# A block of experts computed by 64 rows each with unsplit weights, and a 17th block

## The chip, the core and the metric

The kernel runs on one core of one Trainium2 chip. The metric is the device time of one execution in microseconds (us). TensorE is called PE here, VectorE DVE, ScalarE ACT, GpSimd POOL and SyncE SP; PEld is PE's loading of the stationary operand. SP does nothing but issue DMAs in its order; POOL issues the indirect DMAs and some others.

## The reference

The program computes two transformer blocks over 512 tokens of width 1024 in f32: attention, recurrence and MLP first, then a block with a state-space and sparse-attention mixer. Its last part is the one concerned: a layer of 32 experts (4 groups of 8), of which every token takes two, and a norm. Cut to what matters:

```python
def hier_moe(h, w_group, b_group, w_expert, b_expert, w_gate, w_up, w_down):
    ...
    e_p, e_idx = lax.top_k(jax.nn.softmax(e_logits, axis=-1), TOPK_IN_GROUP)
    w = g_p * e_p / jnp.sum(e_p, axis=-1, keepdims=True)
    eid = g_idx * EXP_PER_GROUP + e_idx
    ...
    def expert_block(args):
        xb, e = args
        return (jax.nn.silu(xb @ w_gate[e]) * (xb @ w_up[e])) @ w_down[e]
    ...
    out = jnp.zeros((N, D), jnp.float32).at[buf_t].add(ys.astype(jnp.float32) * buf_w[:, None])

# second_block, last lines
        h = rms_norm(x, norm2_g[l]) * (1.0 + sc2) + sh2
        x = x + g2 * hier_moe(h, ...)
    return rms_norm(x, final_g)
```

Gate and up are 1024 x 256 for an expert, down is 256 x 1024: 3.1 MB in f32, 100.7 MB for all 32. There are 1024 assignments of a token to an expert. With the given inputs the fullest expert has 85 of them, the next ones 54, 54 and 53.

## The kernel before, in words

The stages run one after the other in one program. The stage before the experts, `output_and_route`, projects the mixer's output, norms each 128 tokens, and routes: the logits, `pick` (the two experts of a token), `table` (the rank of each assignment in its list, and by a product with one-hots the row indices of all lists), `weigh`. The normed tokens are written to DRAM as `h2d` (L1908), from where `gather` (L2260, an indirect DMA on POOL) fetches rows.

*Lists.* Assignments are sorted into 16 lists of up to 128 rows. List p holds the rows of experts p and p+16, mixed; both experts are computed for all 128 rows, and a row's share for each (`share`) makes the other's part zero. What a list cannot hold goes to `overflow`, a loop behind the main part whose count is taken from data; with the given inputs it runs zero times.

*A list.* `rows` transposes its 128 x 1024 inputs (`xT`, L2144). `first` multiplies with gate and up of one expert into `gu` (128 x 512), in units 0 to 3; SiLU (ACT) and a product (DVE) give `mhid`; `turn` transposes it (`hT`, L2181); `second` multiplies by the down weights, units 4 and 5, into the two halves of y, which both experts add to. y is scaled on ACT (L2203) and multiplied by `g2` on POOL (L2204), in the last two lists both on DVE (L2200), and scattered to `yd` in DRAM by an indirect DMA on POOL (L2265). The last list stays on chip.

*Products.* A unit is 128 x 1024 f32, 512 KB, six for an expert, 192 in all. All units but the fourth of an expert are split (`split_w`): ACT casts to fp32r (`wh`, L164), DVE subtracts what is left (L167), and each product is then three matmuls by `TERMS` over halves of x and w (L2160). Unit 3 is multiplied as whole f32 (L2157), which the trace shows as two records for one matmul.

*Weights.* `ahead` issues loads on SP in the order `self.order` into a ring of 25 buffers: 4 `wx`, 5 `wr` and 16 pairs of 128 x 512 scratch tiles (NWX, NWR, NWY); these last are two DMAs of 256 KB each (L2229), the others one of 512 KB (L2231). Every unit taken by `next_w` issues one load more, which waits until its buffer is free: for a split unit that is after its split, for unit 3 after its products. Before the routing ends, 23 units are issued (4, 5, 2 and 12); two of them have been split there by `prepare(2)`. SP then issues the last part of `h2d`, which waits for the norm, and the rest behind it; POOL issues four units between the first two gathers.

*Order and end.* `experts` writes out the order: `first` of the next list stands between the halves of one, so that PE has work while `mhid` and `hT` are made. `side` runs the overflow's table and the last list's row selection on DVE between lists. Behind the last weight loads SP issues the loads of `fg` (L2407) and of the scattered results `yl` (L2414, 16 of 256 KB), which wait for the last scatter; `add_results` adds them to x (L2419, eight on DVE, four on POOL; four go through PE), and `finish` adds the last list by a product with its row selection (L2432 to L2437), norms and stores.

## Time and profile before

| what | us |
|---|---|
| median of 3 runs (lowest, highest) | 2403.62 (2400.61, 2406.93) |
| the profiled execution | 2405.11 |
| its span in the trace | 2403.1 |
| busy: PE, DVE, ACT, POOL | 2276.8, 1489.0, 1125.2, 437.4 |
| granted clock of PE, mean of the span | 0.98 of full speed |
| experts, first products to the last y taken out | 2046.5 to 2374.3 |

The profile is one execution; start times count from its span's start. A busy PE is one with a matmul in it, not one at its peak. A stretch's GB/s counts all that the core's 16 DMA engines moved, and their share is the mean time that they were busy. In the chain of waits each piece is the work, or the DMA, that the next piece waited for. Where an engine's name ends in q, it is the queue that issues.

### The profile page before, as it was taken

What the parts mean: (1) busy time and instruction counts of PE and PEld (TensorE: products, weight loads), DVE (VectorE), ACT (ScalarE), POOL (GpSimd) and SP (SyncE); (2) the same over time, 40 slices, a digit from 0 to 9 for tenths busy, and PEclk for the clock granted to TensorE, in tenths of its full rate; (3) what the DMA queues carried; (4) which work ended last, traced back from release to release, by engine and by line L of the source; (5) the groups of instructions that cost most, each with busy time, mean ns of one, the idle gap of its engine ahead of it and who ended that gap; (6) DMA issues with size and microseconds to landing.
All of it is one profiled execution on the core that took longest, in us unless ns stands there. A gap on an engine that the chain in (4) does not pass through costs nothing.

```text
span 2403.1 us, 33509 instructions
## 1 busy us (share of the span) xinstructions
PE 2276.8 (95%) x12352; PEld 1850.5 (77%) x12352; DVE 1489.0 (62%) x2545; ACT 1125.2 (47%) x2087; POOL 437.4 (18%) x429
## 2 busy tenths in 40 slices
PE   7999989999999999899999998999999997999997
PEld 5887877767888878878888897887788786766664
DVE  7566496555469686753344575343566646888787
ACT  5455553313234375533232352253467723766664
POOL 4001006122015141110000121004000015322221
PEclk9999999999999999999999999999999998999999
DMA  5111256555224312432332236456210066998983
GB/s 180 66 55 57 93 185 221 171 180 173 89 87 140 126 62 97 135 124 97 97 132 91 67 97 202 136 183 227 73 37 2 2 212 227 341 359 309 310 306 116
DMA packets 155534, 352.04 MB, mean 146 GB/s; under 512 B 31089, under 2 KB 42353, under 8 KB 155368
## 3 DMA queue, kind: packets, MB, share of 16 engines
q1 hardware_dynamic: 149816, 337.92, 42.2%
q0 software_dynamic: 5552, 11.95, 1.4%
q8 instruction: 98, 1.61, 0.3%
q14 instruction: 68, 0.56, 0.1%
HBM read 320.56 MB, written 39.31 MB: 150 GB/s over the span
## 4 chain that ended last, share of the span: by engine, by line
PE 53%; DVE 9%; ACT 2%; DMA 2%; issue 2%; POOL 0%; SPq 0%; DVEq 0%; ACTq 0%; POOLq 0%
PE mm L206 25%; PE mm L232 7%; PE gu L2160 4%; PE y L2160 3%; DVE wh L167 2%; PE O L1758 2%; PE S L533 2%; PE PT L587 2%; PE wo L1864 2%; DMA wx<-in_moe_w_dram 1%; PE gu L2157 1%; ACT wh L164 1%; PE mm L209 1%; DVE xc L907 1%; PE hps L1607 1%
## 5 line engine op out<-in xcount | busy, mean ns | idle before, releaser
L167 DVE TENSOR_TENSOR wh<-wr,wh 128x1024 fp32r<-128x1024 f32 x262 | 337.7, 1291 | 442.7 <-ACT wh L164 434.0
L164 ACT CAST wh<-wr 128x1024 fp32r<-128x1024 f32 x274 | 286.9, 1049 | 544.6 <-PE mm L206 391.8
L206 PE MATMUL mm<-xmh,wh 128*128 128x512 f32 x896 | 287.0, 398 | 12.2 <-ACT relu L386 12.2
L206 PE MATMUL mm<-hidh,wh 128*128 128x512 f32 x896 | 289.1, 401 | 3.3 <-DVE m L399 1.9
L167 DVE TENSOR_TENSOR wh<-wx,wh 128x512 fp32r<-128x512 f32 (+1 forms) x261 | 211.5, 851 | 54.7 <-ACT wh L164 50.2
L206 PEld LDWEIGHTS mm<-xmh,wh 128*128 128x128 f32 x896 | 169.8, 190 | 53.5 <-ACT relu L386 15.3
L164 ACT CAST wh<-wx 128x512 fp32r<-128x512 f32 (+1 forms) x261 | 176.1, 717 | 71.7 <-PE y L2160 36.1
L206 PEld LDWEIGHTS mm<-hidh,wh 128*128 128x128 f32 x896 | 168.8, 189 | 47.4 <-ACT wh L164 2.3
L206 PE MATMUL mm<-hidl,wh 128*128 128x512 f32 x448 | 180.0, 402 | 0.0
L206 PE MATMUL mm<-xml,wh 128*128 128x512 f32 x448 | 177.9, 397 | 0.0
L206 PE MATMUL mm<-x2h,wh 128*128 128x512 f32 x512 | 168.2, 400 | 2.4 <-ACT cmpY L1481 1.5
L631 PE MATMUL mm<-x0h,wh 128*128 128x512 f32 x384 | 128.9, 405 | 11.9 <-ACT wh L164 9.5
L2160 PE MATMUL y<-wh,hT 128*128 128x512 f32 x384 | 107.4, 420 | 11.0 <-DVE hT L144 10.5
L267 POOL TENSOR_TENSOR sq<-sq 128x512 f32<-128x512 f32 x12 | 17.8, 1482 | 545.1 <-PE mm L206 318.1
L206 PEld LDWEIGHTS mm<-x2h,wh 128*128 128x128 f32 x512 | 96.4, 189 | 22.4 <-ACT cmpY L1481 2.6
L568 ACT ACTIVATE P<-S,nm 128x128 f32<-128x128 f32 (+3 forms) x192 | 100.5, 535 | 9.6 <-DVE nm L563 9.4
L232 PE MATMUL mm<-xgh,wh 128*128 128x256 f32 x512 | 98.1, 292 | 4.5 <-DVE wh L167 4.5
L206 PEld LDWEIGHTS mm<-hidl,wh 128*128 128x128 f32 x448 | 84.8, 189 | 22.5 <-issue 2.8
L206 PE MATMUL mm<-x2l,wh 128*128 128x512 f32 x256 | 101.9, 398 | 0.0
L2160 PEld LDWEIGHTS y<-wh,hT 128*128 128x128 f32 x384 | 70.9, 190 | 39.9 <-DVE hT L144 16.0
L206 PEld LDWEIGHTS mm<-xml,wh 128*128 128x128 f32 x448 | 85.1, 190 | 19.3 <-issue 2.3
L631 PEld LDWEIGHTS mm<-x0h,wh 128*128 128x128 f32 x384 | 73.3, 192 | 28.3 <-ACT wh L164 9.5
(551 smaller groups left out, 5243.2 us busy)
## 6 DMA issues: line engine op xcount, KB each, us to landing
wx<-in_moe_w_dram SPq DMA_DIRECT2D x236, 256.0 KB
wx<-in_moe_w_dram SPq DMA_DIRECT2D x70, 512.0 KB
wr<-in_mlp_up_dram SPq DMA_DIRECT2D x64, 512.0 KB
wr<-in_mlp_down_dram SPq DMA_DIRECT2D x64, 512.0 KB
wr<-in_ada_w_dram SPq DMA_DIRECT2D x48, 512.0 KB
wr<-in_win_dram SPq DMA_DIRECT2D x40, 512.0 KB
wr<-in_attn_w_dram SPq DMA_DIRECT2D x24, 512.0 KB
wr<-in_rec_w_dram SPq DMA_DIRECT2D x20, 512.0 KB
```

The costliest lines, as they stand in the source:

```text
L164: nc.scalar.copy(out=wh[:, 0, cs], in_=w)
L167: (lo or nc.vector).tensor_tensor(out=wh[:, 1, cs], in0=w, in1=wh[:, 0, cs].bitcast(F32), op=ALU.subtract)
L206: nc.tensor.matmul(out=ps[j], lhsT=wh[:, b, o:o + 128], rhs=X[k][a], start=st, stop=sp)
L209: nc.tensor.matmul(out=ps[j], lhsT=X[k][a][:, j * 128:(j + 1) * 128], rhs=wh[:, b, kk * 512:(kk + 1) * 512], start=st, stop=sp)
L232: mm = nc.tensor.matmul(out=out, lhsT=keep[kb][:, b, o:o + 128], rhs=X[k][a][:, HALF[hf]], start=(k == 0 and n == 0 and j % 2 == 0), stop= ...
L533: nc.tensor.matmul(out=ps, lhsT=q[:, qs], rhs=part[:, 0:N], start=part is k[0], stop=False)
L568: nc.scalar.activation(out=p[:, ns], in_=ps[:, ns], func=AF.Exp, bias=nm[:, o + n:o + n + 1], accum_out=ss[:, o + n:o + n + 1])
L587: nc.tensor.transpose(out=pt[:, c:c + 128], in_=blk[:, kb * 128:(kb + 1) * 128], identity=self.ident)
L631: nc.tensor.matmul(out=ps, lhsT=w[:, b, k * 128:(k + 1) * 128], rhs=X[k][a], start=(k == 0 and n == 0), stop=(k == 7 and n == 2))
L1758: nc.tensor.matmul(out=oo(e), lhsT=V[kb][:, tp * 256 + g * 64:tp * 256 + (g + 1) * 64], rhs=T[2 * m + e][kb], start=False, stop=(tp == 1 a ...
L1864: nc.tensor.matmul(out=ps, lhsT=M[k][a][:, t * 128:(t + 1) * 128], rhs=w[:, b, kk:kk + 512], start=(k == 0 and n == 0), stop=(k == 7 and n ...
L2160: nc.tensor.matmul(out=out, lhsT=x[a][:, cs], rhs=w[:, b, ns], start=start and m == 0, stop=stop and m == 2)
```

## The change

- 64 rows go to each expert of a list: expert p holds rows 0 to 63, expert p+16 rows 64 to 127 (`far` adds the second half's offset, `pk` the list's excess). So a list has one weight per row, and `share` shrinks to one column.
- The weights are no longer split. `product` issues, for each of the two experts, a whole f32 matmul with 64 stationary columns into its half of the output rows; `first` and `second` do both experts together, on one `gu`, one `mhid` and one `hT`.
- An expert with more than 64 rows gets a further block of up to 128 rows. The first such block, "x", is computed as a 17th list after list 12, with six units fetched by 12 indirect DMAs on POOL (`unit_rows`); others would go to the loop. `overflow_list` searches 128 entries rather than 112 and takes 15 steps rather than 7.
- The ring of weight buffers grows by the tiles that held split weights (2 x NWH = 8) to 33. `prepare` is gone, so 21 units are issued before the last part of `h2d`, and 12 more behind it on SP; POOL issues none but those of x.
- y is taken out by DVE in every list.

```diff
-        self.order = list(range(4))
-        for p in range(0, 192, 12):
-            turn = (12, 13, 14, 15, 10, 11) if p < 168 else (10, 11, 12, 13, 14, 15)
-            self.order += [p + u for u in (6, 7, 8, 9, 4, 5, *turn) if p + u < 192]
...
+        self.blocks = list(range(13)) + ["x"] + list(range(13, 16))
+
+        def units(b, us):
+            return [("x", u) for u in us] if b == "x" else [96 * j + 6 * b + u for u in us for j in range(2)]
+
+        self.order = units(self.blocks[0], range(4))
+        for n, b in enumerate(self.blocks):
+            c = self.blocks[n + 1] if n + 1 < len(self.blocks) else None
+            self.order += ([] if c is None else units(c, range(3))) + units(b, (4, 5)) + ([] if c is None else units(c, (3,)))
...
-                self.prepare(2)
                 self.ahead(12)
...
             self.weights_table(self.wtab)
+        self.ahead(self.NWY - 12 + 2 * self.NWH)
...
+        x = hotx.rearrange("p t k e -> p (t k) e")
+        V.tensor_tensor(out=hot.rearrange("p t k e -> p (t k) e"), in0=x[:, :, 0:16], in1=x[:, :, 16:32], op=ALU.add)
+        V.tensor_scalar(out=far, in0=self.ek[:, 2 * t0:2 * (t0 + n)], scalar1=16.0, scalar2=1024.0, op0=ALU.is_lt,
+                        op1=ALU.mult)
...
+        V.scalar_tensor_tensor(out=pk, in0=pe, scalar=64.0, in1=far, op0=ALU.is_ge, op1=ALU.mult)
+        V.tensor_tensor(out=pk, in0=pk, in1=pe, op=ALU.add)
...
-        def products(out, x, c, w, n, start, stop):
-
-            cs, ns = slice(c * 128, (c + 1) * 128), slice(n * 512, (n + 1) * 512)
-            if len(x) == 1:
-                w = w[n] if isinstance(w, list) else w[:, ns]
-                nc.tensor.matmul(out=out, lhsT=x[0][:, cs], rhs=w, start=start, stop=stop)
-                return
-            for m, (a, b) in enumerate(self.TERMS):
-                nc.tensor.matmul(out=out, lhsT=x[a][:, cs], rhs=w[:, b, ns], start=start and m == 0,
-                                 stop=stop and m == 2)
...
+        def product(out, x, c, w, n, start, stop):
+
+            for (a, b), u in zip(parts, w):
+                nc.tensor.matmul(out=out[a:b], lhsT=x[:, c * 128 + a:c * 128 + b], rhs=u[n], start=start, stop=stop)
+
+        def first(q):
+            if q == 0:
                 st["gu"] = self.mm("gu")
...
+            w = [load() for _ in parts]
+            for c in range(2):
+                k = 2 * q + c
+                product(st["gu"], st["xT"][k // 4], k % 4, w, c, k == 0, k == 7)
+            if q == 3:
+                gu, hid = st["gu"], self.s2("mhid")[:, 0:256]
+                st["hid"] = hid
+                nc.scalar.activation(out=hid, in_=gu[:, 0:256], func=AF.Silu)
+                nc.vector.tensor_tensor(out=hid, in0=hid, in1=gu[:, 256:512], op=ALU.mult)
+
+        def turn():
             ps = self.b("hT")
             for c in range(2):
-                nc.tensor.transpose(out=ps[:, c * 128:(c + 1) * 128], in_=st["hid"][j][:, c * 128:(c + 1) * 128],
+                nc.tensor.transpose(out=ps[:, c * 128:(c + 1) * 128], in_=st["hid"][:, c * 128:(c + 1) * 128],
                                     identity=self.ident)
-            hT = self.s2("hT", F32R)
-            st["hT"] = hT[:, 0:256], hT[:, 256:512]
-            self.split(st["hT"], ps[:, 0:256])
-
-        def second(j):
-            if j == 0:
-                st["y"] = [self.mm("y") for _ in range(2)]
+            st["hT"] = self.s2("hT")
+            nc.scalar.copy(out=st["hT"][:, 0:256], in_=ps[:, 0:256])
+
+        def second():
+            ps = [self.mm("y") for _ in range(2)]
             for c in range(2):
-                w = load(False)
+                w = [load() for _ in parts]
                 for h in range(2):
-                    products(st["y"][h], st["hT"], c, w, h, j == 0 and c == 0, j == 1 and c == 1)
-            if j == 1:
-                y = self.c1.tile([128, 1024], F32, name="y", tag="y", bufs=1)
-                for h in range(2):
-                    s = slice(h * 512, (h + 1) * 512)
-                    if soon:
-                        with self.tc.issue_after(self.last_add) if self.last_add is not None else nullcontext():
-                            nc.vector.scalar_tensor_tensor(out=y[:, s], in0=st["y"][h], scalar=share[2],
-                                                           in1=self.g2[:, s], op0=ALU.mult, op1=ALU.mult)
...
-                    nc.scalar.activation(out=y[:, s], in_=st["y"][h], func=AF.Copy, scale=share[2])
-                    nc.gpsimd.tensor_tensor(out=y[:, s], in0=y[:, s], in1=self.g2[:, s], op=ALU.mult)
...
+        def second():
+            ps = [self.mm("y") for _ in range(2)]
             for c in range(2):
+                w = [load() for _ in parts]
                 for h in range(2):
+                    product(ps[h], st["hT"], c, w, h, c == 0, c == 1)
+            y = self.c1.tile([128, 1024], F32, name="y", tag="y", bufs=1)
+            for h in range(2):
+                s = slice(h * 512, (h + 1) * 512)
+                with self.tc.issue_after(self.last_add) if soon and self.last_add is not None else nullcontext():
+                    nc.vector.scalar_tensor_tensor(out=y[:, s], in0=ps[h], scalar=weight, in1=self.g2[:, s], op0=ALU.mult,
+                                                   op1=ALU.mult)
+            done(y)
...
-        m %= self.NWX + self.NWR + self.NWY
+        m %= self.NWX + self.NWR + self.NWY + 2 * self.NWH
         if m < self.NWX:
-            return self.c1.tile([128, 1024], F32, name=name, tag="wx", bufs=self.NWX)
-        if m < self.NWX + self.NWR:
-            return self.wp.tile([128, 1024], F32, name=name, tag="wr", bufs=self.NWR)
-        return [self.s2(name) for _ in range(2)]
+            x = self.c1.tile([128, 1024], F32, name=name, tag="wx", bufs=self.NWX)
+        elif m < self.NWX + self.NWR:
+            x = self.wp.tile([128, 1024], F32, name=name, tag="wr", bufs=self.NWR)
+        elif m < self.NWX + self.NWR + self.NWY:
+            return None, [self.s2(name) for _ in range(2)]
+        else:
+            n = (m - self.NWX - self.NWR - self.NWY) % 2
+            if n == 0:
+                self.pair = self.wp.tile([128, 2, 1024], F32R, name="wh", tag="wh", bufs=self.NWH).bitcast(F32)
+            x = self.pair[:, n]
+        return x, [x[:, 0:512], x[:, 512:1024]]
+
+    def unit_rows(self, idx, u, halves):
+
+        for h in range(2):
+            self.nc.gpsimd.indirect_dma_start(out=halves[h], out_offset=None,
+                                              in_=self.A["moe_w"].rearrange("u p (h c) -> (u p h) c", h=2),
+                                              in_offset=bass.IndirectOffsetOnAxis(ap=idx, axis=0),
+                                              element_offset=u * 128 * 1024 + h * 512)
...
-            if self.unit == 192:
+            if self.unit == len(self.order):
                 return
-            x, src = self.unit_tile(self.unit), self.A["moe_w"][self.order[self.unit]]
+            u, (x, halves) = self.order[self.unit], self.unit_tile(self.unit)
+            self.raw.append(halves)
+            self.unit += 1
+            if isinstance(u, tuple):
+                self.unit_rows(self.xidx[:, 2:3], u[1], halves)
...
-        for p in range(2):
-            self.last_load = self.gather(xg[p], self.idx[:, p:p + 1]).ins
-            if p == 0:
-                self.ahead(self.NWY - 12, nc.gpsimd)
...
+        T, n = [], len(self.blocks)
+        for b in self.blocks:
+            p = 16 if b == "x" else b
+            row = self.xidx[:, 1:2] if b == "x" else self.idx[:, 16 + p:17 + p]
+            done = (lambda y: last.update(y=y)) if b == self.blocks[-1] else (lambda y, row=row: put(row, y))
+            T.append(self.block_tasks(xg[len(T) % 2], ((0, 128),) if b == "x" else ((0, 64), (64, 128)),
+                                      self.share[:, p:p + 1], self.next_w, done, len(T) >= n - 2))
+
+        def fetch(i):
+            b = self.blocks[i]
+            return self.gather(xg[i % 2], self.xidx[:, 0:1] if b == "x" else self.idx[:, b:b + 1])
+
+        for i in range(2):
+            fetch(i)
+        T[0][0]()
+        self.shares(self.wtab[:, 0:32], self.share[:, 0:16])
         nc.sync.dma_start(out=self.g2, in_=self.modrow[3:4].to_broadcast([128, 1024]))
+        for q in range(4):
+            T[0][1](q)
+        add = None
+        for i, (_, first, turn, second) in enumerate(T):
+            if i + 2 < n:
+                fetch(i + 2)
+            if i + 1 < n:
+                rows, ahead = T[i + 1][0:2]
+                rows()
+                ahead(0)
+                ahead(1)
+                turn()
+                ahead(2)
+                second()
+                ahead(3)
+            else:
+                turn()
+                for _ in add:
+                    pass
+                second()
+            if i + 2 == n:
+                for _ in side:
+                    pass
+                add = self.add_results()
+            for _ in range(2):
+                next(side, None)
```

PE in the middle of a list, before. `xTe` and `xTw` are parts of the transposed rows, `wh` split and `wx` whole weights, `mhid` the hidden layer, `hT` its transpose:

```order
L2181 MATMUL hT_18596<-ident_111,mhid_18533 128x128 x2
L2144 MATMUL xT_18606<-ident_111,xg1_16911 128x128 x4
L2144 MATMUL xT_18613<-ident_111,xg1_16911 128x128 x4
L2160 MATMUL gu_18573<-wh_18621,xTe_18404 128x512 x6
L2157 MATMUL gu_18573<-wx_18189,xTw_18405 128x512 x2
L2160 MATMUL y_18639<-wh_18641,hT_18599 128x512 x3
L2160 MATMUL y_18640<-wh_18641,hT_18599 128x512 x3
L2160 MATMUL y_18639<-wh_18652,hT_18599 128x512 x3
L2160 MATMUL y_18640<-wh_18652,hT_18599 128x512 x3
```

The same engine at the `second` of the first list after the change; the even weights are those of expert p, the odd ones of p+16:

```order
L2198 MATMUL y_18430<-wx_18130,hT_18420 64x512
L2198 MATMUL y_18430<-wx_18136,hT_18420 64x512
L2198 MATMUL y_18431<-wx_18130,hT_18420 64x512
L2198 MATMUL y_18431<-wx_18136,hT_18420 64x512
L2198 MATMUL y_18430<-wx_18138,hT_18420 64x512
L2198 MATMUL y_18430<-wx_18165,hT_18420 64x512
L2198 MATMUL y_18431<-wx_18138,hT_18420 64x512
L2198 MATMUL y_18431<-wx_18165,hT_18420 64x512
L2198 MATMUL gu_18401<-wx_18167,xT_18388 64x512
L2198 MATMUL gu_18401<-wx_18175,xT_18388 64x512
L2198 MATMUL gu_18401<-wx_18168,xT_18388 64x512
L2198 MATMUL gu_18401<-wx_18176,xT_18388 64x512
```

Runs of three matmuls by one split weight have become pairs of matmuls of 64 columns by the weights of two experts.

SP at the end of the routing, before; `h2d` is the normed tokens, `g2` the gain of the result:

```order
L2229 DMA wx_17960<-in_moe_w_dram 128x512
L2229 DMA wx_17961<-in_moe_w_dram 128x512
L1908 DMA h2d_17438<-h2_17973 128x512
L1908 DMA h2d_17438<-h2_17974 128x512
L2310 DMA g2_18062<-modrow_3018 128x1024
L2231 DMA wx_18119<-in_moe_w_dram 128x1024
L2231 DMA wx_18127<-in_moe_w_dram 128x1024
L2231 DMA wx_18142<-in_moe_w_dram 128x1024
```

And after, from the end of the units that now follow `h2d`; `wh` are the tiles that were for split weights:

```order
L2280 DMA wx_18068<-in_moe_w_dram 128x512
L2280 DMA wx_18071<-in_moe_w_dram 128x512
L2280 DMA wx_18072<-in_moe_w_dram 128x512
L2277 DMA wh_18075<-in_moe_w_dram 128x1024 x2
L2277 DMA wh_18078<-in_moe_w_dram 128x1024 x2
L2277 DMA wh_18081<-in_moe_w_dram 128x1024 x2
L2277 DMA wh_18084<-in_moe_w_dram 128x1024 x2
L2337 DMA g2_18087<-modrow_3018 128x1024
L2277 DMA wx_18112<-in_moe_w_dram 128x1024
```

Between `h2d` and `g2` stand 12 units that wait for no product.

## Rows read from the trace of the kernel before

**Rows 1.** The page: span, and busy time of each engine.

```profile
span 2403.1 us, 33509 instructions
...
PE 2276.8 (95%) x12352; PEld 1850.5 (77%) x12352; DVE 1489.0 (62%) x2545; ACT 1125.2 (47%) x2087; POOL 437.4 (18%) x429
```

**Rows 2.** Stretches: window, length, busy PE, PEld, DVE, ACT, POOL; clock; DMA; GB/s.

```profile
2037.00:2339.00 302.00, 280.76 (x1162) 203.01 (x1163) 244.36 (x412) 204.11 (x368) 82.18 (x61) 0.97 0.92 324
2046.00:2096.00 50.00, 49.49 (x208) 36.97 (x208) 39.24 (x83) 35.34 (x61) 10.45 (x9) 0.96 1.00 371
2070.00:2080.00 10.00, 10.00 (x49) 7.76 (x48) 7.76 (x32) 7.56 (x16) 5.02 (x4) 1.00 1.05 388
2096.00:2146.00 50.00, 47.42 (x202) 34.43 (x201) 42.47 (x63) 35.08 (x65) 15.93 (x12) 1.00 0.98 338
2339.00:2361.00 22.00, 21.71 (x93) 15.88 (x92) 17.82 (x25) 16.01 (x26) 5.38 (x4) 1.00 0.08 32
```

**Rows 3.** SP's waits, 2046 to 2339: total us, times, longest us.

```profile
SPq L2231 <- DVE wh L167: 33.4, 22, 3.9
SPq L2231 <- PE gu L2157: 33.0, 9, 8.5
```

**Rows 4.** The chain of waits, two places: start us, us, what.

```profile
2042.05 4.34 DMA xg<-h2d,idx
...
2064.99 2.80 PE gu L2160 x12
...
2068.01 1.41 PE gu L2160 x6
2069.42 1.72 PE gu L2157 x4
...
2077.18 0.22 PE hT L2181 x2
2077.40 0.87 PE xT L2144 x8
```

**Rows 5.** The timeline of the tail: start us, us, engine, line, operation.

```profile
2330.28 0.33 SPq L2229 DMA_DIRECT2D wx<-in_moe_w_dram  x1
...
2358.06 1.16 POOL L2265 DMA_INDIRECT yd<-y,idx  x1 [11.05 <-DVE y L2200]
...
2361.50 10.17 SPq L2414 DMA_DIRECT2D yl<-yd  x16
...
2370.90 2.74 DVE L2419 TENSOR_TENSOR h<-h,yl 128x512 f32<-128x512 f32 x4
...
2373.56 0.74 DVE L2200 SCALAR_TENSOR_TENSOR y<-y,share,g 128x512 f32<-128x512 f32 x1
...
2380.25 2.47 DVE L2437 TENSOR_TENSOR h<-h,fin 128x512 f32<-128x512 f32 x4
```

**Rows 6.** The timeline of PE in an earlier stage, the attention.

```profile
1799.82 1.04 PE L1758 MATMUL O<-PTs,v 128*64 128x128 f32 x16
1800.79 1.09 PE L587 MATMUL PT<-ident,P 128*128 128x128 f32 x8
```

**Rows 7.** The timeline at the end of the routing.

```profile
2021.03 1.22 DVE L167 TENSOR_TENSOR wh<-wx,wh 128x1024 fp32r<-128x1024 f32 x1
...
2035.39 1.55 SPq L1908 DMA_DIRECT2D h2d<-h  x2
...
2042.05 1.12 POOL L2260 DMA_INDIRECT xg<-h2d,idx  x1 [5.46 <-DVE half L2038]
```

**Rows 8.** DMA issues from 1940 on: count, median us to landing.

```profile
yd<-y,idx POOLq DMA_INDIRECT x15, 7.6
```

**Rows 9.** Stretches of 2 us around a wait, columns as in rows 2.

```profile
2265.00:2267.00 2.00, 0.79 (x4) 0.56 (x4) 2.00 (x3) 0.19 (x1) 1.86 (x1) 1.00 0.99 342
...
2269.00:2271.00 2.00, 2.00 (x6) 1.60 (x5) 0.67 (x1) 1.60 (x3) 0.00 (x0) 0.50 0.93 332
2273.00:2275.00 2.00, 2.00 (x11) 1.59 (x11) 2.00 (x4) 1.67 (x4) 0.00 (x0) 1.00 0.92 354
```

More of the change, by code (lines that the diff above doesn't have):

```diff
@@ L2136, in rows, with block_tasks @@
+    def block_tasks(self, xg, parts, weight, load, done, soon=False):
+        nc = self.nc
+        st = {}
         def rows():
[L2137 to L2140 removed]
+            st["xT"] = [self.s2("xT") for _ in range(2)]
             for h in range(2):
@@ L2282, in experts, with put @@
         scat = []
-        def put(p, y):
-            st = self.scatter(y, self.idx[:, 16 + p:17 + p])
+        def put(row, y):
+            st = self.scatter(y, row)
             for s in scat:
@@ L2386, in overflow @@
-            self.gather(xg, idx)
-            units = iter(range(12))
-            def load(whole):
-                wr = self.wp.tile([128, 1024], F32, name="wr", tag="wr", bufs=self.NWR)
-                nc.gpsimd.indirect_dma_start(out=wr, out_offset=None, in_=rows,
-                                             in_offset=bass.IndirectOffsetOnAxis(ap=wi, axis=0),
-                                             element_offset=next(units) * 128 * 1024)
-                return wr if whole else self.split_w(wr, 1024)
@@ L2396, in overflow @@
-            res = {}
-            T = self.list_tasks(xg, [share[:, n:n + 1] for n in range(3)], load, lambda y: res.update(y=y), True)
-            for n in ("rows", "first00", "first01", "turn0", "second0", "first10", "first11", "turn1", "second1"):
-                T[n]()
+            idx, weight, sel = self.t([128, 3], "ovi", I32), self.t([128, 1], "ovsh"), self.s2("selT")
+            for _ in self.block_rows(ov, idx, weight, sel):
+                pass
+            self.gather(self.xg[0], idx[:, 0:1])
@@ L2400, in overflow, with load @@
+            units = iter(range(6))
+            def load():
+                return self.unit_rows(idx[:, 2:3], next(units), [self.s2("wx") for _ in range(2)])
+            res = {}
+            rows, first, turn, second = self.block_tasks(self.xg[0], ((0, 128),), weight, load, lambda y: res.update(y=y))
+            rows()
+            for q in range(4):
+                first(q)
+            turn()
+            second()
             self.finish(sel, res["y"])
```

249 lines of the change are left out of this document (94 added, 155 removed).

## The prediction

> **What bounds the kernel now.** Read the busy line first, but only to see that it settles little: TensorE (PE) counts 2276.8 us of a 2403.1 us span [rows 1], an average over stages with different limits. The change lies in the last stage, the experts, so the next view is the table of stretches [rows 2]. Over the 302 us in which the expert weights are loaded beside the products, PE is busy for 280.76 us at a granted clock of 0.97 of 2.4 GHz; the DMA engines have a share of 0.92 and move 324 GB/s. Two resources are close to full. Which one is ahead shows at the edges: in the first 50 us, with the buffers still open, DMA moves 371 GB/s at a share of 1.00, later 338 and less; and when the loads have ended (2339 to 2361), PE goes on for most of 22 us at 21.71 busy. So PE is behind the loads, and the loads are held back by it.
>
> The wait table says the same [rows 3]. SP issues weight loads in order, and each needs a free buffer: in this stage it waits 33.4 us for the DVE subtraction of the weight split (`wh` L167) and 33.0 us for PE (`gu` L2157).
>
> The chain of waits prices PE's work [rows 4]. For one expert of a list: twelve split products 2.80 us, once in `first` and, with the same number, once in `second`; six more in `first` 1.41; and the two products by whole weights 1.72 (four records, two matmuls, so 0.86 us for a whole f32 product over 512 columns). Together 8.73 us. Two experts, one set of eight transposes (0.87) and two pairs of `hT` transposes (0.22 each) make 18.8 us a list. The 16 lists took from 2046.4, where the first rows have landed [rows 4], to 2373.56, where the last y is taken out [rows 5], 20.4 us each; the difference is PE waiting for splits and late weights. The weights of a list are 12 units of 524 KB, 6.29 MB; at 355 GB/s (midway between 338 and 371 of [rows 2]) they need 17.7 us. Today 18.8 of PE stands against 17.7 of DMA.
>
> **The change, part by part.** *Products.* The three fp32r products by split weights go, and so does the computing of both experts over all 128 rows. In their place stand whole f32 products of 64 rows each, two at a time on the two halves of the array: 4 units x 2 plus 2 units x 2, 12 pairs a list. If the pair takes the time of one, a list costs 12 x 0.86 = 10.3 us, plus 0.87 for `xT`, 0.2 for one `hT` and about 0.9 for what opens and closes groups, my allowance: 12.3 us. Does the pair run side by side? The trace has a form like it: `O<-PTs,v`, 64 columns wide in f32, sixteen records in 1.04 us, against eight full-width records in 1.09 us [rows 6]. That is 0.065 us a record against 0.136, and the latency that each row carries once makes the true ratio smaller still. Two half-width products take the time of one, so I take the pair at 0.86; the bound on the other side is 1.72, no overlap (a rival below). That row has 128 moving columns, not 512; nothing suggests that the longer stream differs.
>
> *Splits.* The casts on ACT and the subtractions on DVE of every unit vanish, with them the 33.4 us of SP's wait on L167 [rows 3]; buffers are now freed by the product itself. The evacuation of y, on ACT and POOL before, goes to DVE as two of 0.74 us [rows 5]; DVE gave up far more, so it is hidden.
>
> *The further block.* Blocks of 64 overflow where a list of 128 did not. With the given inputs one expert has 85 rows and the next 54, so the 17th block does work and the loop behind it runs zero times, as before. The block adds 6 units (3.15 MB) and about 12 x 0.86 + 1.1 = 11.4 us of PE. Its weights are fetched by 12 indirect DMAs on POOL's queue. Indirect DMAs issue in about 1.12 us each there [rows 7], some 14 us in all, spread over stretches in which POOL was busy for 82 of 302 us [rows 2]; queued behind them on POOL are only the gather and scatter of neighbouring blocks, two blocks ahead of use. Hidden, as long as PE does not catch up with its buffers; if it is not, about 14 us.
>
> *Bound after.* PE needs 16 x 12.3 + 11.4 = 208 us, and the loads need more, so PE no longer sets the end. I count bytes. Before the routing result (`h2d`) goes out, 21 units are in (23 before). After it SP issues 12 more at once into the enlarged ring of 33, where before it issued nothing and POOL issued four units. `h2d` went out at 2035.39 [rows 7]. Two splits of 1.22 us each leave DVE in the routing; new small DVE operations (wider one-hot, `far`, the correction of `pk`) come to about 0.7 by my count, and not all of either stands on the path: I put the start of unbroken loading at 2035.5. The ring never fills: by 2047, when PE starts, 21 + 7.7 units are in, and PE catches up after some 95 us. From 2035.5 on pass 177 units (92.8 MB), gathers and scatters of about 1024 rows of 4 KB each way (8.4 MB), and `h2d` and `g2` (1.0 MB): 102.2 MB. At 355 GB/s that is 288 us, so the last weight lands near 2323.4, against 2330.28 for its issue today [rows 5], and PE is then at its heels, not 40 us behind. With 338 GB/s the last weight lands at 2337.9, with 371 at 2311.
> *The tail.* The weights of the last block arrive last; the four last units are its down weights. The last unit of the block before lies 6 units ahead of the end, 8.9 us at the rate above, so its y is done (1.7 of PE, 1.5 of DVE) about 5.5 us before the last weight. Its scatter lands 3.4 us after its issue, as the last one today (2358.06 to 2361.50 [rows 5]), when the weights had long ended, or 7.6 as the median under load [rows 8]; I take 5.5, so the 16 loads of the results start as the last weight lands. Eight adds on DVE follow them, four in 2.74 us [rows 5] when nothing is late; with the first load's landing (some 2.5 us, my allowance) they end about 9 us after the last weight, by when y of the last block, 3.5 us after it, is ready. Today from the first `h` L2437 behind the adds, 2380.25, to the end of the span is 22.85 us [rows 1, 5]; none of it changes. So the end is 2323.4 + 9 + 22.85 = 2355.3. The profiled execution took 2405.11, 2.0 outside its span, and lay 1.5 above the median of 2403.62; 2355.3 + 2.0 - 1.5 gives **2356 us**, 48 less than before.
>
> **The rivals.**
> *The loads go no faster than today.* Over the stage they made 324 GB/s; if that is mixing with gathers, and descriptors, rather than waits for buffers, 102.2/0.324 = 315 us, last weight near 2350.5, end at 2382.4, 2383 as a time. For it: the second 50 us with 338 already [rows 2]. Against it: SP's 33.4 and 33.0 us of buffer waits [rows 3] and 371 at a share of 1.00. Chance 0.13.
>
> *The loads go faster.* For ten microseconds the DMA engines moved 388 GB/s [rows 2]; without splits in the way that might hold. 102.2/0.388 = 263.4 us, last weight at 2299, the time 2331; PE, done with its 208 us by 2270 at that pace, would not stop it. Against it: the 50 us around those ten made 371 at a full share, with gathers among them as there will be. Chance 0.08. The Trainium skill, "DMA: Bandwidth & Descriptors", has two figures here: a limit of about 358 GB/s per core under Specifications, and 425 for 16 MB streamed by a core alone under Bandwidth. The trace lies between them, 371 over 50 us and 388 over 10. By 358 the loads would take 285.5 us, 2.5 under mine; by 425 they would take 240.5, and the time would be 2308.
>
> *The two halves do not overlap (slower than before).* If the second of a pair waits for the first, a list costs 24 x 0.86 + 1.1 = 21.7 us, PE is the bound, 16 x 21.7 + 11.4 = 359 us from about 2047 to 2406; then y is taken out (1.5) and the finish runs as today (22.85 and some 2 of its first products), which makes 2432, as a time **2433**. It decides from a pair price of 1.35 us, where PE passes the loads' 17.7 us (12 x 1.35 + 1.5). [rows 6] speak against it. Chance 0.06.
>
> *The clock falls.* Here PE waits for weights in every block. Today's trace shows what a short wait does: with PE busy for 0.79 of 2 us the next stretch but one has a granted clock of 0.50, 1.2 GHz; after busy stretches it is 1.00 again at 2273 [rows 9]. If it stayed at 0.50 for the stage, a block would cost 12 x 1.72 + 2.3 = 22.9 us, above 17.7, and the 17 blocks 388 us: from 2047 to 2435, 2461 at the end. With half the blocks low it is 17 x 20.3 = 345, 2418 at the end; from a third of the blocks on it eats the whole gain. Against it: an engine at the low clock has no gaps left, is busy, and gets the clock back as at 2273; to and fro between 12.3 and 22.9 averages at what the loads allow. The Trainium skill, "TensorE: Matmul & The Clock Gate", HAM oscillation, warns of just this: bursts of matmuls with DMA waits between them drop to the low clock each time, and a kernel can lose much by it; the trace agrees that a wait drops the clock, and shows the recovery beside it. Chance 0.07.
>
> **How the numbers follow.** The forecast has 0.66, faster loads 0.08, the loads at today's rate 0.13, the clock 0.07, no overlap 0.06. The range holds the forecast with both ends of its rate (2311 and 2337.9 for the last weight: 2343 to 2371), the first rival at 2383 and most of the way to the second, so 2333 to 2386; outside lie the slower rivals and half of the faster loads. Within 0.3%, about what a measurement of this kernel can tell from none (7.2 us), I put 0.03; faster 0.66 + 0.08 + 0.12 of the rival with today's rate = 0.86, the 0.01 left of it and 0.02 of the clock in that band; slower 0.06 without overlap + 0.05 of the clock = 0.11.
>
> **What would show it.** Right: pairs of the new product's records starting within some ns of each other, 0.86 us a pair; no `wh` split; DMA share about 1.0 and 338 GB/s or more from 2036 on; PE with gaps ended by `wx` DMAs from about 2140 on, busy some 70%; last weight near 2323; result loads from about then. Wrong: SP still waiting for PE's buffers; a pair at 1.7 us; a clock of 0.5 over whole blocks with PE busy throughout; POOL's indirect fetches, or the blocks' gathers behind them, as what ends PE's waits; a share well under 1.0 while PE waits.

## The result, and the profile after

The changed kernel takes 2343.75 us (median of 4 runs, 2341.44 to 2347.76) against 2403.85 (4 runs, 2400.61 to 2406.93) for the kernel before: a ratio of 0.9752, 95% interval 0.9733 to 0.9770, some 60 us less. The forecast was 2356, within 2333 to 2386. The profiled execution has a span of 2346.0.

The page of the changed kernel, span and busy time, answers to [rows 1]:

```profile
span 2346.0 us, 31955 instructions
...
PE 2196.5 (94%) x12050; PEld 1708.8 (73%) x12050; DVE 1280.1 (55%) x2290; ACT 921.9 (39%) x1737; POOL 396.2 (17%) x410
```

Busy time of PE fell by 80 us, the span by 57: the difference is PE waiting where it did not wait before. The table of stretches shows where, with columns as in [rows 2] (window, length, busy PE, PEld, DVE, ACT, POOL, granted clock, DMA share, GB/s):

```profile
2036.00:2310.00 274.00, 238.73 (x996) 88.65 (x998) 67.77 (x185) 24.12 (x55) 45.08 (x45) 0.94 1.00 373
2108.00:2114.00 6.00, 6.00 (x34) 2.74 (x32) 3.31 (x9) 0.97 (x2) 1.97 (x2) 1.00 1.03 414
2132.00:2138.00 6.00, 5.62 (x31) 2.20 (x27) 2.89 (x7) 0.86 (x2) 1.72 (x2) 1.00 1.03 368
2186.00:2236.00 50.00, 40.10 (x142) 12.30 (x139) 10.96 (x26) 3.70 (x9) 16.95 (x18) 0.97 1.03 391
2282.00:2288.00 6.00, 6.00 (x34) 2.52 (x33) 1.11 (x2) 1.29 (x3) 0.00 (x0) 1.00 0.87 131
2286.00:2310.00 24.00, 22.49 (x107) 7.76 (x105) 4.54 (x7) 2.10 (x5) 1.98 (x2) 1.00 0.93 329
```

The first row is the whole of the loading: a DMA share of 1.00 and 373 GB/s for 274 us, against 0.92 and 324 in [rows 2]. PE is busy for 239 of 274 us and DVE for 68, a quarter of what it was. That is a stage bound by its loads, nearly to its end. The second and third rows are both at a full share and yet move 414 and 368: the loads of whole units and of halves, to which the experiments come back. The fifth is a dip that nobody had in the sum.

SP's waits, 2036 to 2320, to hold against [rows 3]:

```profile
SPq L2280 <- DMA wx<-in_moe_w_dram: 83.8, 136, 3.1
SPq L2277 <- DMA wh<-in_moe_w_dram: 32.1, 31, 2.1
SPq L2277 <- DMA wx<-in_moe_w_dram: 21.7, 41, 1.9
SPq L2277 <- PE gu L2198: 11.8, 8, 5.6
```

SP now waits mainly for earlier weight loads to land, and for buffers held by PE 11.8 us instead of 33.0; the splits' 33.4 are gone with the splits. Waits for earlier loads were there before too, but shorter in sum (2046 to 2339):

```profile
SPq L2229 <- DMA wx<-in_moe_w_dram: 51.9, 106, 2.0
```

The chain of waits in the middle of the stage, which prices the new products as [rows 4] priced the old, and below it the end of the routing:

```profile
2080.88 3.43 PE y L2198 x16
2084.31 1.72 PE gu L2198 x8
```

```profile
2033.13 1.54 SPq L1918 DMA_DIRECT2D h2d<-h  x2
```

Sixteen records in 3.43 us are eight matmuls, four pairs, 0.86 us a pair. That the two of a pair run side by side stands in PE's timeline, where records by the weights of the two experts start within 0.01 us of each other and last 0.59:

```profile
2079.42 0.59 PE L2198 MATMUL gu<-wx,xT 128*64 128x512 f32 x1
2079.43 0.59 PE L2198 MATMUL gu<-wh,xT 128*64 128x512 f32 x1
2079.85 0.59 PE L2198 MATMUL gu<-wx,xT 128*64 128x512 f32 x1
2079.86 0.59 PE L2198 MATMUL gu<-wh,xT 128*64 128x512 f32 x1
```

And the tail, for [rows 5], from the timelines of SP, POOL and DVE:

```profile
2292.85 4.98 SPq L2277 DMA_DIRECT2D wh<-in_moe_w_dram  x8
...
2305.01 0.98 POOL L2294 DMA_INDIRECT yd<-y,idx  x1 [11.13 <-DVE y L2231]
...
2310.76 10.27 SPq L2429 DMA_DIRECT2D yl<-yd  x16
...
2317.31 1.43 DVE L2434 TENSOR_TENSOR h<-h,yl 128x512 f32<-128x512 f32 x2 [1.43 <-DMA yl<-yd]
2318.66 0.75 DVE L2231 SCALAR_TENSOR_TENSOR y<-y,share,g 128x512 f32<-128x512 f32 x1
...
2322.51 1.46 DVE L2452 TENSOR_TENSOR h<-h,fin 128x512 f32<-128x512 f32 x2
```

The last weights were issued by 2297.8 and by the trace's packet records (one for each piece that a DMA engine moved) landed at 2308.2.

### The profile page after: what moved, and what is told of

The parts are those of the page before. It is cut to its first block, busy times and chain, and to the rows that moved or that the text cites. A ratio compares the mean times of both kernels' runs of the same rounds, so it can differ in the third digit from the quotient of the medians.

```text
span 2346.0 us, 31955 instructions
## 1 busy us (share of the span) xinstructions
PE 2196.5 (94%) x12050; PEld 1708.8 (73%) x12050; DVE 1280.1 (55%) x2290; ACT 921.9 (39%) x1737; POOL 396.2 (17%) x410
## 4 chain that ended last, share of the span: by engine, by line
PE 71%; DVE 12%; DMA 9%; ACT 4%; issue 3%; POOL 2%; SPq 1%; DVEq 0%; ACTq 0%; POOLq 0%
PE mm L206 36%; PE mm L232 8%; DMA wx<-in_moe_w_dram 4%; PE mm L631 4%; PE gu L2198 4%; PE S L533 3%; PE PT L587 2%; PE O L1758 2%; DVE wh L167 2%; PE y L2198 2%; DMA wr<-in_ada_w_dram 1%; ACT wh L164 1%; DVE h L329 1%; PE mm L441 1%; PE mm L209 1%
## 5 line engine op out<-in xcount | busy, mean ns | idle before, releaser
L2198 PE MATMUL gu<-wx,xT 128*64 128x512 f32 (+1 forms) x412 | 119.3, 624 | 13.6 <-DMA wx<-in_moe_w_dram 13.1
L206 PEld LDWEIGHTS mm<-x2h,wh 128*128 128x128 f32 x512 | 96.2, 188 | 22.4 <-ACT cmpY L1481 2.7
L2231 DVE SCALAR_TENSOR_TENSOR y<-y,share,g 128x512 f32<-128x512 f32 x34 | 25.5, 751 | 159.2 <-PE y L2198 157.5
L206 PEld LDWEIGHTS mm<-hidl,wh 128*128 128x128 f32 x448 | 84.3, 188 | 21.7 <-issue 2.8
L2198 PEld LDWEIGHTS gu<-wx,xT 128*64 128x64 f32 (+1 forms) x412 | 33.5, 144 | 79.2 <-issue 44.9
L590 ACT COPY PTs<-PT 128x512 f32<-128x512 f32 (+3 forms) x128 | 63.6, 529 | 63.2 <-PE PT L587 62.6
```

What stands on the lines that cost most here:

```text
L206: nc.tensor.matmul(out=ps[j], lhsT=wh[:, b, o:o + 128], rhs=X[k][a], start=st, stop=sp)
L590: nc.scalar.copy(out=sb[:, 0:len(part) * N], in_=pt[:, 0:len(part) * N])
L2198: nc.tensor.matmul(out=out[a:b], lhsT=x[:, c * 128 + a:c * 128 + b], rhs=u[n], start=start, stop=stop)
L2231: nc.vector.scalar_tensor_tensor(out=y[:, s], in0=ps[h], scalar=weight, in1=self.g2[:, s], op0=ALU.mult, op1=ALU.mult)
```

## The experiments

One thing first on how to compare. The code before `h2d` is all but the same in the variants of the changed kernel, yet their profiled executions issued `h2d` anywhere from 2027.5 to 2035.0. So each run has two numbers below: the median time, and in its trace the stretch from `h2d`'s issue to the end of the span, which leaves that out but is one execution. A difference of a few us in this number alone shows little. In these terms the kernel before has 367.7 us (2403.1 - 2035.39 [rows 1, 7]) and the changed kernel 312.9.

| run | median us (runs) | h2d to end, us |
|---|---|---|
| changed kernel | 2343.75 (4) | 312.9 |
| e1_full_width | 2446.06 (2) | 414.5 |
| e2_half_bytes | 2293.37 (2) | 259.1 |
| e3_before_half | 2375.63 (2) | 342.0 |
| e4_no_x | 2335.9 (4) | 301.2 |
| e5_ring25 | 2348.6 (4) | 315.9 |
| e6_x_early | 2345.86 (4) | 313.3 |
| e7_table_row | 2342.92 (4) | 311.0 |
| e8_tail | 2337.96 (4) | 310.6 |
| e9_tail_row | 2337.04 (5) | 307.3 |
| e10_tail_row_x | 2337.31 (4) | 305.2 |
| e11_whole_rows | 2336.9 (5) | 306.7 |
| e12_whole_later | 2329.93 (5) | 297.7 |

**Do the halves run side by side, and do they pay?**

```diff
-            for (a, b), u in zip(parts, w):
-                nc.tensor.matmul(out=out[a:b], lhsT=x[:, c * 128 + a:c * 128 + b], rhs=u[n], start=start, stop=stop)
+            for i, u in enumerate(w):
+                nc.tensor.matmul(out=out, lhsT=x[:, c * 128:(c + 1) * 128], rhs=u[n], start=start and i == 0,
+                                 stop=stop and i + 1 == len(w))
```

> The changed kernel, but each product runs over all 128 rows instead of 64, so the two products of a pair fill the whole array and can't share it: 24 whole f32 products of 128 columns a list, no splits. It leaves out the separation of the two experts, every row gets the sum of both. Theory that the pair runs side by side and the loads are the bound: PE becomes the bound with 24 x 0.86 + 2 = 22.6 us a list, 16 x 22.6 + 12.4 = 374 us from 2048.5, end near 2457 (34.8 us behind the last product as in the changed kernel), time 2440 to 2465. Rival that the halves were not what paid, the missing splits alone were: a time within 10 us of 2344.

2446.06 us, 102 more than the changed kernel and 43 more than the kernel before. Its stretch of 350 us, and DVE's first take of y in two successive lists:

```profile
2050.00:2400.00 350.00, 344.88 (x934) 161.21 (x933) 60.40 (x153) 21.15 (x49) 41.00 (x41) 1.00 0.78 274
```

```profile
2190.81 0.75 DVE L2232 SCALAR_TENSOR_TENSOR y<-y,share,g 128x512 f32<-128x512 f32 x1 [14.29 <-PE y L2198]
...
2213.22 0.75 DVE L2232 SCALAR_TENSOR_TENSOR y<-y,share,g 128x512 f32<-128x512 f32 x1 [14.31 <-PE y L2198]
```

22.4 us a list, PE busy throughout and the loads at 0.78. Without the sharing of the array, whole weights are slower than split ones: the missing splits alone would have lost 43 us. The forecast's rival without overlap had 21.7 us a list and 2433.

**Are the loads the bound after, and were they before?** Both kernels with half the bytes, here the load of a whole unit in the changed one:

```diff
...
-                    load = queue.dma_start(out=x, in_=src)
+                    load = queue.dma_start(out=halves[0], in_=src[:, 0:512])
...
```

> The changed kernel with half of each weight unit loaded (256 KB instead of 512), the loaded half used for both halves; the other half of the weights is left out. PE, DVE and ACT do the same work. Theory that the loads are the bound: PE takes over with about 12.3 us a block, 16 x 12.3 + 12 = 209 us from 2048.5, last product near 2258, time 2285 to 2297. Rival that PE with its clock and its waits is the bound: within 10 us of 2344.

> The kernel before with half of each weight unit loaded, and the loaded half split and used for both halves with instructions of the same size; the other half of the weights is left out. Theory that PE with its splits held the loads back: 18.8 us a list stay, so at most the 1.6 us a list that PE waited go, time 2376 to 2404. Rival that the loads were the bound of the kernel before: some 100 us less, near 2300.

The changed kernel fell to 2293.37, into the range expected of a bound by loads, and PE took over (196.34 busy of 200 us at a clock of 0.99):

```profile
2050.00:2250.00 200.00, 196.34 (x929) 75.19 (x929) 61.24 (x154) 22.71 (x50) 36.07 (x36) 0.99 0.79 258
```

Its lists follow each other in 12.3 us (y taken out at 2144.95 and 2157.22), the 12.3 of the prediction. The kernel before fell by 27.5 us only, to 2375.63, just beyond the good end of what was expected if PE holds the stage; its PE was then busy for 289.64 of 290 us. So before, the late weights cost PE some 1.7 us a list (27.5 over 16) and no more; after, the loads are worth 50 us.

**What does the larger ring do?**

```diff
-        m %= self.NWX + self.NWR + self.NWY + 2 * self.NWH
+        m %= self.NWX + self.NWR + self.NWY
...
-        self.ahead(self.NWY - 12 + 2 * self.NWH)
+        self.ahead(self.NWY - 12)
```

> The changed kernel with the ring of weight buffers as before, 25 units; 4 units instead of 12 are issued behind the routing. Theory that the loads are the bound from the moment the routing ends: they stand still from when the 25th unit is in (about 2042) until the first products free buffers (2051 to 2053), 8 to 11 us, and all of it shows at the end: 2351 to 2355. Rival that the ring's depth buys nothing because PE catches up: 2344, within 2.

5 us more by the medians, 3.0 from `h2d` on; neither theory's number. SP's timeline shows the standstill, and the stretches its size:

```profile
2031.58 3.97 SPq L2280 DMA_DIRECT2D wx<-in_moe_w_dram  x8
2041.18 0.33 SPq L2337 DMA_DIRECT2D g<-modrow  x1
2047.46 8.73 SPq L2277 DMA_DIRECT2D wx<-in_moe_w_dram  x9
```

```profile
2036.00:2046.00 10.00, 6.64 (x26) 4.82 (x28) 3.21 (x16) 2.18 (x4) 3.12 (x3) 0.50 0.75 236
```

SP issued nothing from 2041.5 to 2047.5, but the DMA engines still had queued loads and the first gathers to move, so in those 10 us they lost some 4 us of their full rate, not 8 to 11. What they lost showed at the end.

**What does the 17th block cost?**

```diff
-        self.blocks = list(range(13)) + ["x"] + list(range(13, 16))
+        self.blocks = list(range(16))
```

> The changed kernel without the 17th block: 21 rows of the fullest expert are left out, 6 units (3.15 MB) and 12 indirect loads fewer. Theory that the loads are the bound at 374 GB/s: 3.15 MB plus 1 MB of gather and scatter are 11 us of loading, of which the last part runs into PE's own pace, so 8 to 11 us less than the changed kernel, 2333 to 2336. Rival that the indirect loads on POOL cost more than their bytes (late weights, PE idle, low clock): 15 us or more less, below 2329.

2335.9, 7.9 less; 11.7 from `h2d` on. The expectation counted 128 rows each way for the block, though only its 21 are moved (the packet records of the indirect DMAs from 2036 on hold 11.4 MB here and 8.1 without the block): 3.3 MB are 8.9 us at 374 GB/s, between the two numbers. The indirect loads cost their bytes. They do change the order: POOL issues them as buffers come free, from 2189 on and some 30 units ahead of SP, which has loads of lists 10 to 12 still to issue. DVE's take of y in the changed kernel:

```profile
2224.57 1.61 DVE L2231 SCALAR_TENSOR_TENSOR y<-y,share,g 128x512 f32<-128x512 f32 x2 [12.22 <-PE y L2198]
2252.43 1.61 DVE L2231 SCALAR_TENSOR_TENSOR y<-y,share,g 128x512 f32<-128x512 f32 x2 [19.99 <-PE y L2198]
2266.49 1.58 DVE L2231 SCALAR_TENSOR_TENSOR y<-y,share,g 128x512 f32<-128x512 f32 x2 [9.32 <-PE y L2198]
2278.84 1.61 DVE L2231 SCALAR_TENSOR_TENSOR y<-y,share,g 128x512 f32<-128x512 f32 x2 [7.20 <-PE y L2198]
2291.00 1.61 DVE L2231 SCALAR_TENSOR_TENSOR y<-y,share,g 128x512 f32<-128x512 f32 x2 [7.61 <-PE y L2198]
```

These are lists 10, 11, 12, x and 13. List 11 is 27.9 us behind list 10, and what follows comes every 12.2 to 14.1 us, PE's pace: weights were lying ready. The long gap itself is not x's doing: without the block, in e4, list 11 is 25.0 us behind list 10 (2215.25 and 2240.29) and the next two follow in 14.4 and 12.0. What opens it is not shown. What x adds is time and backlog: lists 9 to 11 take 69.1 us together, 61.5 in e4, and after them four lists come at PE's pace rather than two. From 2252 on PE, not the loads, sets the rhythm, which is why the last stretch of the table above has PE at 22.49 of 24.

**The end: backlog, dip and tail.** Three edits, each alone.

```diff
-        self.blocks = list(range(13)) + ["x"] + list(range(13, 16))
+        self.blocks = list(range(8)) + ["x"] + list(range(8, 16))
```

> The changed kernel with the 17th block after list 7 instead of list 12, nothing else. In the changed kernel lists 13 to 15 follow each other in 12.3 us, PE's pace, because the loads of x ran ahead of list 12's and left a backlog. Theory that this backlog delays the end: with x earlier PE has caught up by the end, the second last list's y is done 2 to 3 us earlier against the last weight, time 2340 to 2342. Rival that only the sum of the bytes counts: 2344, within 1.5.

2345.86, and 313.3 from `h2d`: no gain. The backlog went (the last lists are 16.1 to 21.4 us apart), and the scatter left 5.55 us before the last weight landed (2299.88 and 2305.43) instead of 3.2, as the theory has it. But the last weight landed 277.5 us after `h2d` instead of 275.1, in the one execution of each that can be read, and ate that. The theory's step is seen; that it moves the end is not shown.

```diff
-        self.ovd = self.dp.tile([14, 128, 2], F32, name="ovd")
-        nc.sync.dma_start(out=self.ovd.rearrange("n p k -> p n k"), in_=ov[:, 2:30].rearrange("p (n k) -> p n k", k=2))
+        self.ovd = self.dp.tile([14, 2], F32, name="ovd")
+        nc.sync.dma_start(out=self.ovd.rearrange("(o n) k -> o (n k)", o=1), in_=ov[0:1, 2:30])
...
```

> The changed kernel with the overflow table written to DRAM from one partition (one piece of 112 bytes) instead of 1792 pieces of 8 bytes from 128 partitions. In the changed kernel the DMA engines moved 131 GB/s in the 6 us in which those pieces passed. Theory that they block the weight loads, which are the bound: 4 us less, 2338 to 2341. Rival that the lost bytes are made up because PE has a backlog there: 2344, within 1.5.

The dip is gone, but the median is 2342.92, within the rival's 1.5. Where the table passed, PE was at work without a gap on its backlog:

```profile
2272.00:2296.00 24.00, 23.95 (x110) 8.82 (x106) 5.23 (x8) 2.69 (x6) 2.00 (x2) 1.00 1.00 358
```

```diff
...
+            if n + 2 == len(self.blocks):
+                self.order += units(b, (4, 5)) + units(c, range(4))
+                continue
...
                 rows()
+                if i + 2 == n:
+                    turn()
+                    second()
                 ahead(0)
...
```

> The changed kernel with the down weights of the second last list loaded and used before the last list's gate and up, so its scatter leaves 6 units earlier. Theory that the loads of the results, which wait for this scatter, set the end: they start as soon as SP has issued the last weights, and the DMA engines don't pause between; 4 to 6 us less, 2338 to 2340. Rival that the last list's own y and the finish set it: 2344, within 1.5, or later by the 2 us in which PE waits for hT.

2337.96, 5.8 less (from `h2d` on only 2.3, in the slowest of its four executions). The scatter now leaves at 2300.87. SP had issued the last weights by 2300.0 and then waited for the scatter's landing, 6.9 us in the chain of waits, so the 16 loads of the results did not follow the weights' issue at once. But they were issued at 2307.90, before the last weights landed at 2310.5, and the DMA engines did not pause (a share of 1.04 from 2292 to 2320):

```profile
2300.87 6.89 DMA yd<-y,idx
...
2307.90 5.09 DMA yl<-yd
```

Beside the table this execution had a stretch worse than that of the changed kernel:

```profile
2284.00:2290.00 6.00, 6.00 (x30) 2.01 (x28) 0.00 (x0) 0.00 (x0) 0.00 (x0) 1.00 0.68 54
```

Together:

> The changed kernel with two of the edits together: the second last list's down weights before the last list's gate and up, and the overflow table as one piece of 112 bytes. Alone they gave some 6 and 1 us by the medians; in the trace of the first, 6 us of loading at 54 GB/s beside the table remained. Theory that both act on the same line of loads and add up: 4 to 6 us less than the first edit alone, 2331 to 2335. Rival that the finish (products, norm and stores behind the last y) sets the end by now: 2338, within 1.5.

> The same two edits, and the 17th block after list 7. Theory that only the sum of the bytes counts, as x moved alone showed (2 us more by the medians, 0.4 more from the routing's end): the same as the two edits alone, within 2. Rival that the backlog behind list 12 shows now that the end is shorter: 2 to 4 us less.

2337.04 and 2337.31. From `h2d` on they are 3.3 and 5.4 us shorter than e8, by the medians not measurably, so the sum of both that e9's theory expected did not come; that the place of x adds nothing, as e10's theory has it, holds by the medians. The trace of e9 shows where it went: its last weight landed 270.3 us after `h2d`, in e8 278.8, but PE, on its backlog, was so late with the second last list that its scatter left at 2297.99, behind that weight (2297.8), and the loads of the results were issued at 2300.78. So in that execution PE held the end. That the finish did, the rival's reason, does not fit e12 below, which is faster with the same finish. What the dip costs by itself the runs leave open.

**What sets the rate of the loads?** Units in the ring's whole buffers have rows of 4 KB, those in pairs of tiles rows of 2 KB.

```diff
...
+        if m >= self.NWX + self.NWR + self.NWY + 2 * self.NWH:
+            m = (m - 33) % 17
+            m += 16 * (m >= self.NWX + self.NWR)
...
```

(and `next_w` issues nothing for a unit taken from a pair)

> The two edits, and from the 34th unit on the weights go only into the 17 whole buffers, one DMA of 512 KB with 4 KB a row each, and no longer into pairs of 128 x 512 tiles with 2 KB rows. In the trace of the changed kernel the stretches of whole units moved 414 GB/s and those of pairs 368 to 374, both at a full DMA share. Theory that the row's length sets the rate: the loads that are left run at some 410, 15 to 18 us less, and SP stands still some 10 us once, while the pairs of the first round are used without being filled again; 5 to 8 us less than the two edits alone. Rival that the rate differs for another reason, or that 17 buffers are too few: 8 us more or worse.

2336.9, as e9, and so neither the 5 to 8 us less of the theory nor the 8 more of the rival. The rate rose as the theory has it, and the standstill was dearer:

```profile
2062.00:2086.00 24.00, 23.98 (x126) 9.56 (x124) 8.97 (x37) 2.68 (x6) 4.04 (x4) 1.00 0.56 202
2086.00:2136.00 50.00, 48.45 (x214) 18.30 (x211) 11.35 (x27) 3.92 (x9) 7.06 (x7) 1.00 1.03 410
2136.00:2186.00 50.00, 45.91 (x171) 15.15 (x170) 13.01 (x30) 3.70 (x9) 6.04 (x6) 1.00 1.02 402
```

In 24 us at 202 instead of 400 GB/s some 12 us of loading are lost, where 10 were expected; that leaves some of the missing gain without a cause. The last run keeps the pairs for three rounds and drops them from the 100th unit on, when PE waits for loads anyway (`if m >= 99: m = (m - 99) % 17`), with x early, the table as a row and the tail's order:

> As the kernel with whole rows, but the pairs of 128 x 512 tiles stay in the ring for three rounds, until PE has caught up with the loads, and only from the 100th unit on the weights go into whole buffers alone; the 17th block after list 7. In the kernel with whole rows from the 34th unit on the loads ran at 395 to 410 GB/s, but stood still once (66 GB/s over 12 us) and lost there what they had won. Theory that the standstill came from PE using up the pairs while it was faster than the loads: no standstill now, half of the later loads at 400 instead of 370, 3 to 5 us less than the two edits with x early, 2332 to 2335. Rival that 17 buffers are too few at any time: 2337 or more.

2329.93 (2327.34 to 2331.81), 7.4 less than the same without whole rows (6.4 if each is taken from the kernel before as timed beside it) and under the range expected: 13.8 under the changed kernel, a ratio of 0.9696 to the kernel before (0.9682 to 0.9709). Against e10 the same 50 us, first e12, then e10:

```profile
2186.00:2236.00 50.00, 44.81 (x183) 15.42 (x178) 12.63 (x29) 3.81 (x9) 6.09 (x6) 1.00 1.01 402
```

```profile
2186.00:2236.00 50.00, 43.62 (x176) 14.69 (x173) 12.63 (x29) 3.43 (x8) 6.08 (x6) 1.00 0.99 372
```

The last weight landed 267.2 us after `h2d`, in e10 272.6. Is it the row's length? In these runs the size of a DMA changes with it (one of 512 KB against two of 256), and so does the number of buffers in use, so the runs don't separate them. The packet records of the weight loads speak for a part: in the changed kernel the median packet of 4 KB took 159 ns and that of 2 KB 84, so two short ones take 168.

## Why the prediction was right, and where its sizes were off

*What bounds the kernel.* Right: PE before (e3), the loads after (e2). Of the signs named, PE's gaps ended by `wx` began at 2132.8 instead of 2140, and PE was busy 80% of the time from 2186 to 2236 instead of 70%. *The pair at 0.86.* Right, 3.43 us for four pairs; the row of the attention [rows 6] carried over from 128 moving columns to 512. A block at 12.3 us was 12.3. The rival without overlap was added up with 1.1 us beside its products where the forecast has 2.0; e1, whose products can't overlap, has 22.4 us a list, 1.8 beside 24 x 0.86. *Splits and y hidden.* Right: DVE is busy for a quarter of the stage. *The further block hidden.* Right in that it costs its bytes. That its loads are issued on another queue, ahead of those of lists 10 to 12, was not seen; PE then paced the last four blocks, where without the block it paced two after the same gap.

*Bytes.* 102.2 MB were counted; the packet records hold 102.3 from 2034.8 to the last weight's landing at 2308.2. *The start.* 2035.5 was taken, `h2d` went out at 2033.13 and the weights behind it from 2034.8. How much of that is the missing splits can't be told, since this moment varies by 7 us between executions.

*The rate.* This is the term that was mis-sized. The step was "355 GB/s (midway between 338 and 371 of [rows 2])". Measured were 374, 273.4 us instead of 288. In the span, 2346.0 against 2355.3 of the sum, that is -14.6, with -0.7 from the start and +6 from the tail below. That the tail's error is of the other sign and hides part of the rate's is luck. The median then lay 4.0 under the profiled execution (2347.76), where 1.5 was taken from the kernel before. The 338 of the second 50 us was taken for what the engines can do, at a share of 0.98; what held it there is not shown. The two rates by row length could hardly have been read from the trace before: 388 GB/s in 2070 to 2080 [rows 2] are pairs with short rows, and whole units made 401 in the best 6 us (here the second line) but 362 in the 10 us around them:

```profile
2130.00:2140.00 10.00, 9.96 (x45) 7.18 (x44) 6.81 (x10) 7.04 (x12) 2.67 (x2) 1.00 0.98 362
2132.00:2138.00 6.00, 5.96 (x24) 4.11 (x23) 4.58 (x7) 4.30 (x8) 0.67 (x1) 1.00 1.02 401
```

The rival with 388 was too fast, that with 324 too slow. Both figures of the Trainium skill, "DMA: Bandwidth & Descriptors", Specifications and Bandwidth, are off as a mean for this stage, 358 under and 425 over; 414 in six microseconds of whole units, and 410 over 50 us of them in e11, come near the upper one.

*The tail.* The last weight to the end was put at 9 + 22.85 = 31.9 us and took 37.8. The scatter left 3.2 us before the last weight, not 5.5, because PE was on its backlog (in e6, without it, 5.55); it landed in 5.7 (5.5 was taken); then the adds ended 11.8 us after the first load's issue, not 9: the 4.2 MB of the results came in at 325 GB/s (2312 to 2323, a share of 0.92), and DVE waited 9.3 us for them. The finish itself took 23.5 against 22.85.

*The clock.* The rival with the low clock did not come, and for the reason given. While PE waited for loads in every list, from 2186 to 2236, it had 40.10 busy of 50 us and a clock of 0.97. Between 2060 and 2310 it fell to 0.50 (1.2 GHz) three times and came back each time: near 2201, behind 10 us with 6.16 busy; near 2242, where PE stood still for 4.8 us before list 12's products; and near 2256, behind a wait of 1.9 us for DVE:

```profile
2191.00:2201.00 10.00, 6.16 (x17) 1.10 (x13) 0.00 (x0) 0.00 (x0) 4.19 (x5) 1.00 1.04 392
2201.50:2204.90 3.40, 3.27 (x8) 1.10 (x10) 0.00 (x0) 0.00 (x0) 0.00 (x0) 0.51 1.04 413
...
2240.00:2245.00 5.00, 0.38 (x1) 0.00 (x0) 0.00 (x0) 0.00 (x0) 0.00 (x0) 0.75 0.98 342
2245.00:2250.00 5.00, 4.82 (x12) 2.37 (x14) 0.00 (x0) 0.15 (x1) 0.00 (x0) 0.57 0.96 346
...
2255.00:2260.00 5.00, 4.68 (x14) 2.57 (x15) 1.60 (x5) 0.58 (x1) 1.33 (x2) 0.66 1.03 412
2260.00:2262.00 2.00, 2.00 (x8) 0.99 (x7) 0.00 (x0) 0.00 (x0) 0.00 (x0) 1.00 1.03 408
```

With the first products, which ran at 0.50 until 2054.8, the mean clock from 2036 to 2310 was 0.94. The example in the Trainium skill, "TensorE: Matmul & The Clock Gate", HAM oscillation, in which the clock drops at every wait for data, has waits that are longer than the products between them. In the lists from 2186 to 2236 the waits were the shorter part, 9.9 of 50 us, and the clock fell there once, not at each wait.

## What to carry to other kernels

Where two resources are both above nine tenths, price the second one as carefully as the first: once PE was relieved, the rate of the loads decided most of the time, and it was guessed as a midpoint. Small-batch experts can share the array, two of 64 rows each; without that, unsplit f32 weights are dearer than three split products (e1). When loads are the bound, look at the length of their rows, at the size of their DMAs and at what else rides on the queues before moving instructions about.

## What was not expected of the hardware

At a full DMA share, loads with rows of 4 KB, in DMAs of 512 KB, moved 402 to 414 GB/s (the changed kernel and e11); those with 2 KB rows, in DMAs of 256 KB, moved 368 in the changed kernel (2132 to 2138) and 388 in the one before (2070 to 2080). Sending half of the later loads with the longer rows gave 7.4 us (e12 against e10); which of row, DMA size and number of buffers gave it the runs don't separate. And 1792 pieces of 8 bytes, 14 KB in all, beside the loads went with a fall to 131 GB/s over 6 us in the changed kernel and to 54 in e8; with one piece in their place e7 kept 358 over the 24 us around it. What it costs in time the runs leave open.
